# Side tasks of a hybrid decoder step: other waiting counts, earlier SSD blocks, gates one at a time, a fifth score buffer

## The chip, the cores and the metric

One core of a Trainium2 chip runs the whole kernel. The core has a matrix engine (TensorE, PE in the rows), two elementwise engines (VectorE, DVE, and ScalarE, ACT), GpSimd (POOL), and a queue engine (SyncE, SP) that issues nearly all DMAs. The metric is the device time of one execution in microseconds (us); the kernel before took 1676.14 us, the median of three runs from 1675.15 to 1676.15.

## The reference, cut to what matters

A decoder trunk of two layers in float32 handles a prompt of 1024 tokens and one new token for each of 8 samples. In each layer the residual x feeds one input projection whose outputs go to three mixers, and one output projection and a layer norm close the layer:

```
proj = x @ w_in            # 1024 -> 4876 columns
att  = sliding-window attention (window 128, 8 query heads, 2 key heads, sinks, partial rotary)
hl   = RG-LRU: conv(4) -> r, i = sigmoid(block matmuls) -> h_t = a_t h_{t-1} + b_t
y    = Mamba-2 SSD: conv(4)+silu on x, B, C -> chunked scan (chunks of 128) + D*x
y    = y * silu(z); y = y * rsqrt(mean(y^2)) * norm_g
out  = concat(att*silu(g_att), hl*silu(g_lru), y) @ w_out
x    = layer_norm(alpha * x + out)
```

The caches and states after the step are outputs too.

## The kernel before, in words

The work is done in four steps: for each of two layers, first half 0 (512 prompt tokens), then half 1 (512 prompt tokens and the 8 samples, 520 columns in two chunks of 260). Tokens lie along the free dimension and channels on partitions. A step projects 38 blocks of 128 output channels (`project`), then adds up the output projection in four groups of input rows (`out_proj`).

Every large product is taken as three float32r matmuls (`mac3`, lines 299 to 301: high weights by high x, high weights by low x, low weights by high x). These are the main products. ACT makes the high part of each weight tile (`wh`, lines 249 and 251), POOL the low part (`wl`, line 253); in half 1 the low part is read back from DRAM (`low`).

Everything else is a side task: a Python generator that emits some instructions and then yields a number. `pump()` is called once per slot, that is after every 12 main products in half 0 and every 24 shorter ones in half 1; it counts each task down and lets it emit its next piece when the count is used up. So a `yield 3` puts three slots of main products between two pieces of a task. `drain(...)` pumps without main products until the named streams are empty. What the generators emit is then placed on each engine by a scheduler that may shift instructions by some places; each engine runs its own list in order.

The side tasks that the change touches:

- Attention, `block` (line 845 on): scores into a `sp` tile (L855, L856 on PE, L859 on DVE, L863 on ACT), three slots, transposes (L873) and their copy into a second `sp` tile (L876 on DVE or L878 on ACT), one slot, then the product with the values (L884). `sp` has four buffers (`NS2`). `attention_sample` does the same for the samples (transposes of cached keys at L935).
- SSD step sizes, `rest` in `ssd_steps`: a cumulative sum (L539, L540), its negation on DVE (L543, tile `acs`), one slot, then its transpose on PE (L552), on which all SSD blocks rest.
- SSD, `block(g, b)` in `ssd_stream`: for each of two groups and four chunks, transposes (L627), decays (L643 on ACT, L644 on POOL, L650 on ACT, L652 on DVE, from a tile `acr` that a DMA broadcasts out of DRAM), three slots, the state and output products (L655, L660), and `finish` (L600, L602 on DVE), which multiplies with the z gate. A group starts when its block 7 has been projected: blocks 0 to 2 are x, 3 is B, 4 is C, 5 to 7 are the z gates. At the end the sums of squares (L613, L614), a reciprocal (L738) and six scalings (L742).
- RG-LRU, `lru_stream`: for each of six tiles the two gates on PE (L457) and ACT (L459), an elementwise chain (L464 to L485), and the product with the output gate. A tile starts only when its output gate (`g_lru`) is projected.
- `prepare_ssd`, `prepare_lru`, `past_rows`: tables of per-channel parameters, loaded once.

PSUM is evicted by DVE in the output projection (L1024) and for gates (L346), by ACT elsewhere (L332). Main products use three PSUM buffers (`ip`), side products five (`mm`). Large SBUF tiles (`u`) come from ten buffers; x, the mixers' inputs and the inputs of the output projection (`load_mix`, L229 on ACT and L230 on DVE) share them.

Of the kernel before, what the change touches and what calls it, by code (L numbers as in the profile page):

```python
# [14 lines left out]
ALU = mybir.AluOpType  # L15
AX = mybir.AxisListType

P = 128
# [14 lines left out]
LS = 41  # L33
SS = 29
NH = 5
NS2 = 4
# [14 lines left out]
def tile_trunk(ctx, tc, outs, x_t, cache_k, cache_v, st_lru_conv, st_ssd_conv, st_ssd_h, w_in, w_dt, w_out,  # L51
# [120 lines left out]
    def prepare_ssd():  # L172
        dma(ssd_p, ssd_cols)
        dma(dcol, ssd_d)
        for l in range(LAYERS):
            o = l * SS + 24
            V.tensor_scalar(ssd_p[:, :, o:o + 5], ssd_p[:, :, o:o + 5], 0.5, None, op0=ALU.mult)
        past_rows(past_s, ssd_p, 10, SS, 24)
# [11 lines left out]
    def prepare_lru():  # L190
        dma(lru_p, lru_cols)
        past_rows(past_l, lru_p, 6, LS, 32)

        spt = ctile([P, 5, 6 * LAYERS], "spt")
        lam = ctile([P, 6 * LAYERS], "lam")
        for l in range(LAYERS):
            o = l * LS + 37
            V.tensor_scalar(lru_p[:, :, o:o + 2], lru_p[:, :, o:o + 2], 0.5, None, op0=ALU.mult)
            V.tensor_scalar(lam[:, 6 * l:6 * l + 6], lru_p[:, :, l * LS + 39], -1.0, None, op0=ALU.mult)
# [168 lines left out]
    def past_rows(out, prm, n, per, wo):  # L368

        tmp = wtile([P, 10, NS], "sd", ND)[:, :n]  # L370
        for l in range(LAYERS):
            for t in range(3):
                to = out[:, l] if t == 0 else tmp
                V.tensor_tensor(to, prm[:, :, l * per + t:l * per + t + 22:3],
                                prm[:, :, l * per + wo + t, None].to_broadcast([P, n, NS]), ALU.mult)
                if t:
                    V.tensor_tensor(out[:, l], out[:, l], tmp, ALU.add)
# [34 lines left out]
    def lru_project(st, l, half, x, j, what):  # L412
# [6 lines left out]
        for i in range(3):  # L419
            t = 3 * j + i  # L420
            if what == 0:
                ps = project(l, x, W, B_XL + t)
                conv(ps, half, W, lru_p[:, t, :], l * LS + 32, past_l[:, l, t, :], halo_l[:, t, :], xc[:, i, :W],
# [11 lines left out]
    def lru_stream(st, l, half, mixrows):  # L435
# [3 lines left out]
        for j in range(2):  # L439
# [3 lines left out]
            yield 2  # L443
            xc = st["xc", j]
            for i in range(3):
                while ("lru", j, 1, i) not in st:
                    yield 1
                t = 3 * j + i
                gate = st["gt", j][:, i, :W]
                r, ig = wtile([P, WMAX], "hb", NH), wtile([P, WMAX], "hb", NH)  # L450
                for gi, dst in ((0, r), (1, ig)):
                    for cs in chunks(W):
                        ps = mm_tile()
                        n = cs.stop - cs.start
                        for k, c0, c1 in ((i, 0, 32), (i, 32, 64), (i, 64, 96), (3, 96, P)):
# [4 lines left out]
                                     bias=lru_p[:, t, o + 37 + gi:o + 38 + gi])  # L460
# [14 lines left out]
                if half:  # L475
                    V.tensor_tensor(t2[:, HALF:W], t2[:, HALF:W], lru_p[:, t, o + 24:o + 32], ALU.mult)
# [13 lines left out]
    def ssd_steps(st, l, half, x):  # L490
# [12 lines left out]
        def rest():  # L503
# [46 lines left out]
            yield 1  # L550
# [10 lines left out]
    def ssd_project(st, l, half, x, g, i):  # L561
# [6 lines left out]
        if i < 5:  # L568
# [3 lines left out]
            conv(ps, half, W, ssd_p[:, t, :], l * SS + 24, past_s[:, l, t, :], halo_s[:, t, :], dst,  # L572
# [17 lines left out]
    def ssd_stream(st, l, half, mixrows):  # L590
# [4 lines left out]
        def finish(g, cs, wd, yps):  # L595

            xb, zc = st["xb", g], st["zc", g]
            yd = wtile([P, 3, P], "sd", ND)
            for i in range(3):
                V.scalar_tensor_tensor(yd[:, i, :wd], xb[:, i, cs], dcol[:, l, 3 * g + i:3 * g + i + 1],  # L600
                                       yps[:, i, :wd], op0=ALU.mult, op1=ALU.add)
            V.tensor_tensor(zc[:, 0:3, cs], yd[:, :, :wd], zc[:, 0:3, cs], ALU.mult)  # L602
            left[g] -= 1
# [12 lines left out]
        def block(g, b):  # L616
# [53 lines left out]
            finish(g, cs, P, py[:, :384].rearrange("p (i q) -> p i q", i=3))  # L670

        def sample(g):
# [29 lines left out]
            finish(g, cs, NS, ysum)  # L702
# [29 lines left out]
        squares(1)  # L732
        for cs in chunks(W):
# [5 lines left out]
        for t in range(6):  # L739
            g, i = divmod(t, 3)  # L740
            zt = st["zc", g][:, i, :W]
            V.scalar_tensor_tensor(zt, zt, lru_p[:, t, l * LS + 40:l * LS + 41], ssq[:, :W],  # L742
# [95 lines left out]
    def attention_stream(st, l, half, mixrows, mixd0):  # L838
        W = HALF + NS * half

        def block(g, b, qa, ga):
# [37 lines left out]
            yield 1  # L879
# [30 lines left out]
        if half:  # L910
            spawn("att", keys_out())
            spawn("att", attention_sample(l, st["qs"], st["k_last"][:, P:], st["tab"][:, 2, :], st["gas"], mixd0))

    def attention_sample(l, qs, kn, vT, gas, mixd0):
# [7 lines left out]
        yield 1  # L922
# [8 lines left out]
        for i in range(2):  # L931
            kcT.append(wtile([P, 4, P], "sp", NS2))
# [355 lines left out]
```

## Time and profile before

| | before |
|---|---|
| median of three runs | 1676.14 us |
| the profiled execution | 1670.71 us, of it 1669.0 us from the first to the last instruction (the span) |
| mean granted TensorE clock | 0.976 of full |
| PE, DVE, ACT, POOL busy | 94%, 64%, 58%, 39% of the span |
| main products | 7776 of 10696 matmuls |
| DMA | 202 GB/s mean over the span |

A row of a timeline gives the start, the duration, the engine, the line, the operation, the output and inputs by the program's names, the shapes, a count, and in brackets how long the engine had been idle and what ended that. A PE record is longer than the time that a matmul takes of a stream, since records overlap; the rate is read from how many start in a stretch.

### The profile page before, as it was taken

The numbers are of one execution on the slowest core, as the hardware profiler recorded it, in microseconds if no ns is written. First come the engines' busy times: TensorE is split into PE (matmuls) and PEld (weight loads), VectorE is DVE, ScalarE is ACT, GpSimd is POOL, SyncE is SP. The second block draws the span as 40 slices with busy tenths as digits, with TensorE's granted clock in tenths as the row PEclk, the third lists the DMA queues.
The fourth block names the chain that finished last, engine by engine and source line by source line (L and its number), as shares of the span: only waits on it lengthen the run. The fifth ranks groups of instructions, "written<-read, shape, count | busy, mean of one in ns | idle before, by whom it ended". The sixth has DMA issues, their size and how long they took to land. (4 is left out here: it accounts for less than half of the span.)

```text
span 1669.0 us, 30988 instructions
## 1 busy us (share of the span) xinstructions
PE 1573.8 (94%) x10696; PEld 1340.7 (80%) x10696; DVE 1071.9 (64%) x2206; ACT 976.2 (58%) x2144; POOL 650.3 (39%) x858
## 2 busy tenths in 40 slices
PE   8999999999989999989998999988999998999996
PEld 6677776578989887879976777665899997978896
DVE  5656567855854766775488665679436557677734
ACT  5655566833555646783256564667346656578724
POOL 5654766463021354400155555665512105352000
PEclk9999999999989999999999999999999999999998
DMA  8655555986554666687546555568865556676965
GB/s 277 192 172 162 164 167 159 310 267 192 169 176 148 210 199 185 208 278 261 190 135 218 180 155 151 155 188 303 267 217 191 159 169 204 187 211 186 326 202 197
DMA packets 210660, 337.43 MB, mean 202 GB/s; under 512 B 24116, under 2 KB 64000, under 8 KB 210456
## 3 DMA queue, kind: packets, MB, share of 16 engines
q1 hardware_dynamic: 208200, 331.27, 62.5%
q10 hardware_dynamic: 2304, 4.20, 0.7%
q8 instruction: 84, 1.38, 0.3%
q14 instruction: 72, 0.59, 0.1%
HBM read 242.76 MB, written 92.05 MB: 201 GB/s over the span
## 5 line engine op out<-in xcount | busy, mean ns | idle before, releaser
L299 PE MATMUL ip<-u,wh 128*128 128x260 f32 (+3 forms) x2592 | 852.2, 329 | 31.6 <-DVE u L1024 15.1
L301 PE MATMUL ip<-u,wl 128*128 128x260 f32 (+3 forms) x2592 | 838.3, 325 | 13.2 <-DMA wl<-low 7.8
L300 PE MATMUL ip<-u,wh 128*128 128x260 f32 (+3 forms) x2592 | 838.1, 324 | 0.0
L299 PEld LDWEIGHTS ip<-u,wh 128*128 128x128 f32 x2592 | 495.9, 191 | 90.8 <-DVE u L1024 19.7
L301 PEld LDWEIGHTS ip<-u,wl 128*128 128x128 f32 x2592 | 494.2, 191 | 58.3 <-POOL wl L253 10.6
L300 PEld LDWEIGHTS ip<-u,wh 128*128 128x128 f32 x2592 | 496.3, 191 | 38.7 <-issue 3.2
L253 POOL TENSOR_TENSOR wl<-wraw,wh 128x256 fp32r<-128x256 f32 x432 | 374.1, 890 | 279.2 <-ACT wh L251 190.0
L249 ACT ACTIVATE wh<-wraw 128x512 fp32r<-128x512 f32 x224 | 138.7, 627 | 160.5 <-PE ip L300 130.2
L251 ACT ACTIVATE wh<-wraw 128x512 fp32r<-128x512 f32 x216 | 134.7, 627 | 148.5 <-PE ip L300 79.3
L1024 DVE SCALAR_TENSOR_TENSOR u<-u,ip 128x260 f32<-128x260 f32 (+3 forms) x192 | 96.7, 510 | 149.0 <-PE ip L301 147.3
L362 DVE SCALAR_TENSOR_TENSOR u<-ev,ssd_p,u 128x512 f32<-128x512 f32 x120 | 98.3, 820 | 19.2 <-ACT u L354 18.3
L863 ACT ACTIVATE sp<-sp,mx 128x257 f32<-128x257 f32 (+1 forms) x128 | 62.6, 491 | 42.6 <-DVE mx L859 42.6
L643 ACT ACTIVATE cq<-acr 128x384 f32<-128x384 f32 x56 | 29.2, 522 | 99.1 <-DMA acr<-acsd 88.7
L644 POOL TENSOR_TENSOR cq<-cq,u 128x384 f32<-128x384 f32 x56 | 63.8, 1140 | 51.7 <-ACT cq L643 33.4
L650 ACT ACTIVATE acr<-acr,acs 128x128 f32<-128x128 f32 x192 | 63.2, 393 | 33.5 <-POOL acr L647 30.7
L230 DVE TENSOR_TENSOR u<-u 128x512 fp32r<-128x512 f32 (+1 forms) x88 | 66.9, 785 | 17.6 <-ACT u L229 17.4
L362 DVE SCALAR_TENSOR_TENSOR u<-ev,lru_p,u 128x512 f32<-128x512 f32 x72 | 60.9, 846 | 24.8 <-ACT u L354 24.5
L229 ACT ACTIVATE u<-u 128x512 fp32r<-128x512 f32 (+1 forms) x88 | 52.3, 626 | 33.1 <-DMA u<-xd 14.9
L332 ACT ACTIVATE ev<-ip 128x260 f32<-128x260 f32 (+2 forms) x132 | 58.4, 443 | 17.9 <-PE ip L301 17.5
L457 PE MATMUL mm<-u,gw 96*32 96x260 f32 (+1 forms) x576 | 56.1, 468 | 13.4 <-ACT q L634 7.4
L652 DVE TENSOR_TENSOR acr<-acr,q 128x384 f32<-128x384 f32 x64 | 40.8, 669 | 42.2 <-ACT q L638 28.5
L859 DVE CUSTOM_DVE_ANT_0 sp<-mm,amask,sp 128x256 f32<-128x256 f32 (+1 forms) x128 | 54.6, 463 | 11.7 <-PE mm L856 10.5
(280 smaller groups left out, 2125.0 us busy)
## 6 DMA issues: line engine op xcount, KB each, us to landing
wraw<-in_w_in_dram SPq DMA_DIRECT2D x304, 256.0 KB
wl<-low SPq DMA_DIRECT2D x224, 256.0 KB
low<-wl SPq DMA_DIRECT2D x216, 256.0 KB
wraw<-in_w_out_dram SPq DMA_DIRECT2D x136, 256.0 KB
acr<-acsd SPq DMA_DIRECT2D x64, 192.0 KB
u<-mixd SPq DMA_DIRECT2D x32, 260.0 KB
u<-mixd SPq DMA_DIRECT2D x32, 256.0 KB
mixd<-u SPq DMA_DIRECT2D x24, 260.0 KB
```

The lines of the kernel that those rows point to most:

```text
L230: V.tensor_tensor(dl, raw, dh.bitcast(F32), ALU.subtract)
L249: S.activation(h, raw, AF.Copy)
L251: S.activation(h, raw, AF.Copy)
L253: G.tensor_tensor(low[:, c], raw[:, c], h[:, c].bitcast(F32), ALU.subtract)
L299: PE.matmul(out, wh, xh, start=first, stop=False)
L300: PE.matmul(out, wh, xl, start=False, stop=False)
L301: PE.matmul(out, wl, xh, start=False, stop=last)
L362: V.scalar_tensor_tensor(out[:, :HALF], raw[:, t:t + HALF], prm[:, wo + t:wo + t + 1], out[:, :HALF], op0=ALU.mult, op1=ALU.add)
L644: G.tensor_tensor(cq[i], cq[i], zc[:, None, 3, cs].to_broadcast([P, 3, P]), ALU.mult)
L650: S.activation(acr[i][:, e, :], acr[i][:, e, :], AF.Exp, scale=-1.0, bias=nacs[:, eb + 3 * i + e:eb + 3 * i + e + 1])
L863: S.activation(s[:, kv, :nk + 1], s[:, kv, :nk + 1], AF.Exp, scale=-1.0, bias=mx[:, kv:kv + 1], accum_out=den[:, kv:kv + 1])
L1024: V.scalar_tensor_tensor(ro, ro, ALPHA if gi == 0 else 1.0, out, op0=ALU.mult, op1=ALU.add)
```

## The change

Seven edits go together.

- Waiting counts: L552 comes 3 slots after L543 instead of 1 (in layer 1, half 0, the order has 36 main products between L540 and it, before 22); the value product L884 2 slots after the transposes instead of 1; the samples' transposes 4 slots after `prod` instead of 1, with a slot between the two key halves; `keys_out` starts after 8 slots instead of 3; RG-LRU waits 3 slots for its gate weights instead of 2; the mean square's product comes 2 slots after the last squares.
- SSD blocks of a group start at block 5 (x, B and C projected) instead of block 7. `finish` is cut in two: `weighted` right after the product, and the multiplication with z once block 7 is there. In layer 0, half 0, the last SSD products stand 48 main products earlier in PE's order.
- RG-LRU tiles start without their output gate and wait for it at the last product.
- The two gates of a tile are emitted one slot apart, and 3 slots (not 4) follow the tile.
- `NS2` is 5.
- The conv states' rows are no longer kept in SBUF with the parameters: `channel_rows` loads them into scratch (`hb`) tiles, in two parts for SSD and one for RG-LRU, and copies the parameters out. This frees 3072 bytes per partition (288 and 480 float32 columns).
- Line numbers differ: 299 to 301 are 295 to 297 in the changed kernel, 457 is 459, 229 is 225, 251 is 247, 655 and 660 are 667 and 672, 742 is 761, 346 is 342.

```diff
-NS2 = 4
+NS2 = 5
@@ prepare_ssd, prepare_lru
-        dma(ssd_p, ssd_cols)
...
-        past_rows(past_s, ssd_p, 10, SS, 24)
+        channel_rows(ssd_cols, 10, SS, 0, 0.5, ssd_p, past_s)
...
-        dma(lru_p, lru_cols)
-        past_rows(past_l, lru_p, 6, LS, 32)
+        channel_rows(lru_cols, 6, LS, 8, 1.0, lru_p, past_l)
@@
+    def channel_rows(cols, n, per, wo, scale, prm, past):
+        m = n if n * LAYERS * (ROWS + per) <= WMAX else n // 2
+        for t0 in range(0, n, m):
+            ts = slice(t0, t0 + m)
+            raw = wtile([P, WMAX], "hb", NH)[:, :m * LAYERS * (ROWS + per)].rearrange("p (t c) -> p t c", t=m)
+            dma(raw, cols[:, ts, :])
+            tmp = wtile([P, m, NS], "sd", ND)
...
@@ lru_stream
             dma(gw, gates_w[l, j])
-            yield 2
+            yield 3
             for i in range(3):
-                while ("lru", j, 1, i) not in st:
-                    yield 1
...
+                    if gi == 0:
+                        yield 1
...
+                while ("lru", j, 1, i) not in st:
+                    yield 1
+                gate = st["gt", j][:, i, :W]
                 V.scalar_tensor_tensor(gate, r, 0.5, gate, op0=ALU.mult, op1=ALU.mult)
-                yield 4
+                yield 3
@@ ssd_steps, rest
             V.tensor_tensor(dd, dd, dt[:, :48], ALU.mult)
-            yield 1
+            yield 3
@@ ssd_stream
-            finish(g, cs, P, py[:, :384].rearrange("p (i q) -> p i q", i=3))
+            yd = weighted(g, cs, P, py[:, :384].rearrange("p (i q) -> p i q", i=3))
+            while ("ssd", g, 7) not in st:
+                yield 1
+            finish(g, cs, P, yd)
...
-            while "steps" not in st or ("ssd", g, 7) not in st:
+            while "steps" not in st or ("ssd", g, 5) not in st:
                 yield 1
...
         squares(1)
+        yield 2
@@ attention
-            yield 1
+            yield 2
             po = mm_tile()
...
-            spawn("att", keys_out())
+            spawn("att", keys_out(), 8)
...
         V.tensor_tensor(prod, qs, kn[:, :, None].to_broadcast([P, NS, 8]), ALU.mult)
-        yield 1
+        yield 4
...
         for i in range(2):
+            yield 1
             kcT.append(wtile([P, 4, P], "sp", NS2))
```

What is executed stays the same but for 14 more small DVE instructions and one more DMA in the preparation, and 8 fewer table loads on ACT. The order moves. Three places follow, first before and then changed.

ACT, layer 0, half 0, before the output projection. L229 (225) is the first group's input (`u<-u`), L251 (247) the high weights, L613 (625) the SSD squares, L345 (341) the gates' evictions, L459 (461) to L469 (473) the RG-LRU chain. Before:

```order
L354 ACTIVATE u<-ev,lru_p 128x512
L229 ACTIVATE u<-u 128x512 x4
L251 ACTIVATE wh<-wraw 128x512
L613 ACTIVATE ev<-u 128x512 x3
L251 ACTIVATE wh<-wraw 128x512
L345 ACT_TABLE_LOAD
L345 ACTIVATE ev<-ip 128x512
```

Changed:

```order
L625 ACTIVATE ev<-u 128x512 x3
L247 ACTIVATE wh<-wraw 128x512
L328 ACTIVATE ev<-ip 128x512
L350 ACTIVATE u<-ev,lru_p 128x512
L247 ACTIVATE wh<-wraw 128x512 x2
L328 ACTIVATE ev<-ip 128x512
L350 ACTIVATE u<-ev,lru_p 128x512
L756 ACTIVATE ssq<-mm,eps_t 128x512
```

The squares stood behind L229 and now stand ahead of it, 18 rows before L225 x4, and the root of their sum (L756) with them.

PE, layer 0, half 0, the second RG-LRU tile. L457 (459) are the gates, the rest main products or SSD products. Before:

```order
L300 MATMUL ip<-u,wh 128x512
L301 MATMUL ip<-u,wl 128x512
L457 MATMUL mm<-u,gw 32x512 x8
L299 MATMUL ip<-u,wh 128x512
L300 MATMUL ip<-u,wh 128x512
L301 MATMUL ip<-u,wl 128x512
```

Changed, from the second gate on (the first stands 12 main products earlier, as another x4):

```order
L296 MATMUL ip<-u,wh 128x512
L297 MATMUL ip<-u,wl 128x512
L459 MATMUL mm<-u,gw 32x512 x4
L667 MATMUL mm<-sd,q 128x384
L672 MATMUL mm<-cq,hst_115 64x128 x2
L672 MATMUL mm<-acr,sd 64x128 x2
```

One group of eight became two of four. Over the whole program there are 27 such rows before and 48 after.

DVE, layer 0, half 1, around the start of the output projection. L742 (761) are the SSD scalings, L346 (342) the gates' evictions, L468 (472) to L485 (492) the RG-LRU chain, L1024 (1044) the evictions of the output projection. Before:

```order
L738 RECIPROCAL ssq<-ssq 128x520
L346 SCALAR_TENSOR_TENSOR u<-ev,ip 128x260
L742 SCALAR_TENSOR_TENSOR u<-u,lru_p,ssq 128x520 x6
L470 SCALAR_TENSOR_TENSOR hb<-hb,u 128x520
L468 SCALAR_TENSOR_TENSOR hb<-hb 128x520
L471 SCALAR_TENSOR_TENSOR hb<-hb 128x520
L346 SCALAR_TENSOR_TENSOR u<-ev,ip 128x260 x2
```

Changed:

```order
L757 RECIPROCAL ssq<-ssq 128x520
L358 SCALAR_TENSOR_TENSOR u<-ev,lru_p,u 128x512
L761 SCALAR_TENSOR_TENSOR u<-u,lru_p,ssq 128x520 x6
L474 SCALAR_TENSOR_TENSOR hb<-hb,u 128x520
L389 COPY q<-mm 66x128
L358 SCALAR_TENSOR_TENSOR u<-ev,lru_p,u 128x512
L472 SCALAR_TENSOR_TENSOR hb<-hb 128x520
L475 SCALAR_TENSOR_TENSOR hb<-hb 128x520
L342 SCALAR_TENSOR_TENSOR u<-ev,ip 128x260 x2
```

The scalings stand among the RG-LRU convolutions (L358) instead of between evictions of the last output gates.

## Rows read from the trace of the kernel before

**Rows 1.** The page, busy time by engine: us, share, instructions
```profile
PE 1573.8 (94%) x10696; PEld 1340.7 (80%) x10696; DVE 1071.9 (64%) x2206; ACT 976.2 (58%) x2144; POOL 650.3 (39%) x858
```

**Rows 2.** Clock of the core: span, mean granted share
```profile
core 0: 1669.0 us, clock 0.976
```

**Rows 3.** Waits of PE: instruction, releaser, us in total, times, longest
```profile
PE ip L299 <- DVE u L1024: 15.1, 12, 4.3
PE ip L299 <- ACT wh L251: 10.3, 4, 6.5
PE mm L884 <- ACT sp L878: 8.8, 3, 3.4
PE ip L301 <- DMA wl<-low: 7.8, 5, 2.9
PE mm L457 <- ACT q L634: 7.4, 4, 2.9
PE mm L457 <- DMA u<-u: 5.5, 3, 2.7
PE mm L552 <- DVE acs L543: 5.5, 2, 4.4
PE ip L301 <- POOL wl L253: 5.1, 4, 2.4
PE ip L299 <- DVE u L346: 4.7, 3, 2.3
PE mm L935 <- DVE sp L876: 3.4, 2, 2.2
```

**Rows 4.** Stretches: length, busy us (count) of each engine, PE clock, DMA
```profile
0.00:20.00 20.00, 13.49 (x47) 9.82 (x48) 11.50 (x24) 13.33 (x33) 13.12 (x32) 1.00 0.91 305
...
280.00:300.00 20.00, 16.16 (x64) 10.70 (x63) 13.08 (x18) 14.48 (x22) 10.22 (x10) 0.83 0.55 179
...
360.00:380.00 20.00, 20.00 (x88) 16.11 (x87) 4.82 (x7) 4.43 (x7) 9.51 (x14) 1.00 0.74 223
...
880.00:900.00 20.00, 15.58 (x61) 12.56 (x61) 19.12 (x39) 9.93 (x26) 9.39 (x12) 0.83 0.70 240
...
1400.00:1420.00 20.00, 13.20 (x107) 10.84 (x106) 16.33 (x49) 13.27 (x34) 11.29 (x14) 0.91 0.71 208
```

**Rows 5.** Timeline of PE from 281 to 288 us
```profile
283.84 0.50 PE L299 MATMUL ip<-u,wh 128*128 128x512 f32 x1 [1.47 <-ACT wh L251]
...
286.95 0.79 PE L301 MATMUL ip<-u,wl 128*128 128x512 f32 x1 [2.37 <-POOL wl L253]
```

**Rows 6.** Timeline of ACT from 262 to 287 us
```profile
281.08 2.19 ACT L229 ACTIVATE u<-u 128x512 fp32r<-128x512 f32 x4 [4.21 <-DVE sd L600]
```

**Rows 7.** Timeline of DVE from 270 to 287 us
```profile
280.71 0.34 DVE L600 SCALAR_TENSOR_TENSOR sd<-u,dcol,mm 128x128 f32<-128x128 f32 x1
```

**Rows 8.** Timeline of PE from 879 to 886 us
```profile
884.60 0.41 PE L552 MATMUL mm<-ident,acs 128*48 128x128 f32 x1 [4.42 <-DVE acs L543]
```

**Rows 9.** Timeline of DVE from 877 to 886 us
```profile
884.34 0.20 DVE L543 TENSOR_SCALAR acs<-mm 128x48 f32<-128x48 f32 x1
```

**Rows 10.** Waits of ACT: the longest sum with a DMA
```profile
ACT cq L643 <- DMA acr<-acsd: 88.7, 28, 6.7
```

**Rows 11.** Groups of ACT by line and shape: busy us, mean ns, idle before
```profile
L857 ACT ACTIVATE sp<-sink_bc 128x2 f32<-128x2 f32 x64 | 12.6, 198 | 0.6 <-PE mm L884 0.4 <-DVE sink_bc L136 0.2
```

**Rows 12.** Timeline of PE from 1491 to 1500 us
```profile
1491.24 0.28 PE L301 MATMUL ip<-u,wl 128*128 128x260 f32 x1
1491.45 1.52 PE L457 MATMUL mm<-u,gw 96*32 96x260 f32 x24
1495.85 0.65 PE L457 MATMUL mm<-u,gw 96*32 96x260 f32 x8 [2.88 <-ACT q L634]
1496.42 0.39 PE L299 MATMUL ip<-u,wh 128*128 128x260 f32 x1
```

**Rows 13.** Timeline of DVE from 716 to 739 us
```profile
735.78 0.70 DVE L468 SCALAR_TENSOR_TENSOR hb<-hb 128x520 f32<-128x520 f32 x1 [2.53 <-ACT hb L466]
```

More of the change, by code (lines that the diff above doesn't have):

```diff
@@ L32 @@
 B_K, B_V, B_Q, B_GA, B_XL, B_GL, B_Z, B_XBC = 0, 1, 2, 6, 10, 16, 22, 28
-LS = 41
-SS = 29
+LS = 17
+SS = 5
+ROWS = 24
 NH = 5
-NS2 = 4
+NS2 = 5
 NE = 5
@@ L172, in prepare_ssd @@
     def prepare_ssd():
-        dma(ssd_p, ssd_cols)
+        channel_rows(ssd_cols, 10, SS, 0, 0.5, ssd_p, past_s)
         dma(dcol, ssd_d)
-        for l in range(LAYERS):
-            o = l * SS + 24
-            V.tensor_scalar(ssd_p[:, :, o:o + 5], ssd_p[:, :, o:o + 5], 0.5, None, op0=ALU.mult)
-        past_rows(past_s, ssd_p, 10, SS, 24)
         G.memset(tri, 1.0)
@@ L366, in conv @@
             G.tensor_copy(last, raw[:, HALF:HALF + 11])
[L368 to L377, printed above, removed]
+    def channel_rows(cols, n, per, wo, scale, prm, past):
[5 more added lines that the diff above has]
+            tmp = wtile([P, m, NS], "sd", ND)
+            for l in range(LAYERS):
+                r0 = l * (ROWS + per)
+                V.tensor_scalar(prm[:, ts, l * per:(l + 1) * per], raw[:, :, r0 + ROWS:r0 + ROWS + per], scale, None,
+                                op0=ALU.mult)
+                for t in range(3):
+                    to = past[:, l, ts] if t == 0 else tmp
+                    V.tensor_tensor(to, raw[:, :, r0 + t:r0 + t + 22:3],
+                                    prm[:, ts, l * per + wo + t, None].to_broadcast([P, m, NS]), ALU.mult)
+                    if t:
+                        V.tensor_tensor(past[:, l, ts], past[:, l, ts], tmp, ALU.add)
     def rows_out(src, m, dsts):
@@ L422, in lru_project @@
                 ps = project(l, x, W, B_XL + t)
-                conv(ps, half, W, lru_p[:, t, :], l * LS + 32, past_l[:, l, t, :], halo_l[:, t, :], xc[:, i, :W],
+                conv(ps, half, W, lru_p[:, t, :], l * LS + 8, past_l[:, l, t, :], halo_l[:, t, :], xc[:, i, :W],
                      last_l[:, :, t])
@@ L571, in ssd_project @@
             ps = project(l, x, W, ssd_block(g, i))
-            conv(ps, half, W, ssd_p[:, t, :], l * SS + 24, past_s[:, l, t, :], halo_s[:, t, :], dst,
+            conv(ps, half, W, ssd_p[:, t, :], l * SS, past_s[:, l, t, :], halo_s[:, t, :], dst,
                  last_s[:, :, t])
@@ L593, in ssd_stream, with weighted @@
         left = {}
-        def finish(g, cs, wd, yps):
-            xb, zc = st["xb", g], st["zc", g]
+        def weighted(g, cs, wd, yps):
+            xb = st["xb", g]
             yd = wtile([P, 3, P], "sd", ND)
@@ L601, in finish @@
                                        yps[:, i, :wd], op0=ALU.mult, op1=ALU.add)
+            return yd
+        def finish(g, cs, wd, yd):
+            zc = st["zc", g]
             V.tensor_tensor(zc[:, 0:3, cs], yd[:, :, :wd], zc[:, 0:3, cs], ALU.mult)
@@ L701, in sample @@
                 yield 1
-            finish(g, cs, NS, ysum)
+            while ("ssd", g, 7) not in st:
+                yield 1
+            finish(g, cs, NS, weighted(g, cs, NS, ysum))
         def final_state(g):
@@ L741, in ssd_stream @@
             zt = st["zc", g][:, i, :W]
[L742 removed]
+            V.scalar_tensor_tensor(zt, zt, lru_p[:, t, l * LS + 16:l * LS + 17], ssq[:, :W],
                                    op0=ALU.mult, op1=ALU.mult)
@@ L931, in attention_sample @@
         for i in range(2):
+            yield 1
             kcT.append(wtile([P, 4, P], "sp", NS2))
```

9 lines of the change are left out of this document (4 added, 5 removed).

## The prediction

> **What bounds the kernel now.** The page comes first: PE is busy 94% of the span, the next engine 64% [rows 1]. So the end is set by PE's stream, and an edit counts only where it closes a hole in that stream or lengthens it. What an undisturbed stream does is in the table of stretches: from 360 to 380 us PE starts 88 products of 512 columns, one in 0.227 us, at the full clock [rows 4]. A slot of 12 is therefore 2.7 us. From 1400 to 1420 us it starts 107 matmuls and is busy only 13.2 us [rows 4]: one of the holes.
>
> Who makes the holes is in the list of PE's waits [rows 3]. They fall into five kinds, and only four have to do with this change: weights that ACT and POOL finish late (L251, L253), the transpose of the SSD sums (L552), products whose operand has just been copied (L884, L935), the RG-LRU gates (L457), and PSUM evictions that DVE does late (L1024, L346). The low weights from DRAM (7.8 us) wait for a transfer that nothing here moves. Of the 10.3 us for L251, the longest, 6.5 us, is the start of the program, when PE has nothing to do yet.
>
> A hole costs twice. In the stretch from 280 to 300 us, which holds two weight waits, the granted clock is 0.83, from 880 to 900 us, after a wait of 4.42 us, 0.83, from 1400 to 1420 us 0.91 [rows 4, 8]. There are two levels, 2.4 and 1.2 GHz, so 0.83 over 20 us is 6.8 us at the lower one, and what the stream loses is at most (1 - 0.83) x 20 = 3.4 us; at 0.91 it is 1.8 us. Over the span (1 - 0.976) x 1669 = 40 us is the most that all of this can be [rows 2]; I use 1.8 to 3.4 us for each hole that closes.
>
> **The change part by part**, against the profiled execution (1670.7 us; the median of the runs is 5.4 us above it, and I add that at the end).
>
> *SSD blocks start earlier (weights at the output projection).* At 281 us ACT has stood idle for 4.21 us in front of L229, the input of the output projection [rows 6]. What it waited for is L600, which ends at 281.05 us [rows 7]: the tile that L229 writes is the SSD input that L600 still reads. Behind L229 in ACT's order stands L251, the high weights, and PE then waits 1.47 us for them and 2.37 us for the low part that POOL makes of them [rows 5]. In the new order the last SSD products of this half stand 48 main products earlier, 48 x 0.227 = 10.9 us, which is more than the 4.21 us; the tile is free when L225 comes. Both layers have this place: without the program's start, [rows 3] has 10.3 - 6.5 = 3.8 us for L251 and 5.1 us for L253, together 8.9 us, and two drops of the clock. What is late next: the RG-LRU chain, which I leave in the last term. Between 0 and 8.9 + 5.2 = 14.1 us; I take 11.
>
> *Three slots before the SSD transpose.* DVE works through a queue of long normalisation steps and comes to L543 at 884.34 us; PE, which stands at L552, waits 4.42 us, with all main products behind it [rows 8, 9]. Now 36 main products instead of 22 lie between: 14 x 0.227 = 3.2 us, and the score products that stand there too are some more. Of the two waits (5.5 us in all [rows 3]), the short one goes, the long one shrinks to about 1 us, and the clock stays: 1.1 + 3.2 + 2.4 = 6.7 us. The blocks that rest on this transpose start up to 2 slots later, which the earlier start of the groups hides; without that cover it would take back the 2.7 to 5.4 us.
>
> *One slot more before L884, and between the samples' pieces.* Three waits of L884, 8.8 us, the longest 3.4 us, and two of L935, 3.4 us [rows 3]. A slot takes 2.7 us from each: 8.8 would shrink to about 1.4 us, L935 to nothing. That would be 10.8 us and three drops of the clock, 16 us. But what makes ACT late is not distance alone: it stands in front of L643 for the broadcast of `acr` 88.7 us in all, up to 6.7 us at a time [rows 10], and the change leaves that DMA in the same step as its reader; SP issues it earlier together with its block, past weight loads. So between 0 and 16 us; I take 9. The fifth score buffer is priced at nothing: the instruction that opens a new score tile (L857) waited 0.4 us for L884 with four [rows 11], and with tiles held one slot longer the fifth keeps it there.
>
> *Gates one at a time, tiles without their output gate.* The waits are 7.4 us for L634, which empties a PSUM buffer that the gates need, and 5.5 us for the shifted rows (`u<-u`) [rows 3]. One more slot before the first gate is 2.7 us against a longest wait of 2.7 us; half as many PSUM buffers are asked for at once. With some four drops of the clock the most is 12.9 + 8 = 21 us. ACT's order is still that of [rows 10], so I take half, 10.4 us.
>
> Against it stands a sure cost. A gate's chunk is 8 records. The last one alone, from its start to the next main product, takes 1496.42 - 1495.85 = 0.57 us; three of them (24 records) start 1491.45 us and, at the same rate with one exit, give about 0.44 us each, so leaving costs 0.13 us; entering takes 0.21 us (1491.24 to 1491.45) instead of 0.12 us [rows 12]. Each extra group is 0.22 us; the order has 48 instead of 27: 21 x 0.22 = 4.6 us. Bounds: 0 (where the group stands beside SSD products that change the shape anyway) and 21 x 0.57 = 12 us.
>
> The Trainium skill has a rule here: "TensorE: Matmul & The Clock Gate", Part 3, says that packed small matmuls take the duration of one plus about 4 ns for each further tile, and names no cost of entering or leaving; by it the split would cost nothing and the sum would be 4.6 us better. The rows above show the entry and the exit as time, so they decide.
>
> *Evictions.* DVE does the six SSD scalings, the RG-LRU chains and the evictions L346 and L1024 in one queue at the start of the output projection. At 735.78 us it stands 2.53 us for ACT in front of L468, with L1024 behind it [rows 13], and the longest wait of PE for L1024 is 4.3 us; L1024 and L346 together make 19.8 us [rows 3]. In the new order the scalings are done among the convolutions, before the output gates. But the RG-LRU chain ends later, since a tile now takes the same slots and its start is bound by the tile before; L472 still stands in front of L1044. Between -5 (the chain meets more of the evictions) and 19.8 + 4 = 24 us; I take half, 12.
>
> *Preparation.* 14 more small DVE instructions and one more DMA; at 0.20 us for a small one [rows 9] 2.8 us. In the first 20 us DVE is busy 11.5 us [rows 4], so they hide; 0, at worst 2.8.
>
> *New waits.* In half 1 the samples' SSD work of group 0 now falls on the last attention groups, where it did not before. From 1400 to 1420 us, where such work met before, PE lost 6.8 us [rows 4]. No row shows the new meeting; between 0 and two such holes (13.6 us and clock 3.6) I take 7 for the two layers, one half of a hole each.
>
> Sum: 11 + 6.7 + 9 + 10.4 + 12 - 4.6 - 7 = 37.5 us; 1670.7 - 37.5 = 1633, and with the 5.4 us to the median 1638 us.
>
> **The rivals.**
>
> *Only the certain part comes.* Waits on ACT and DVE are waits on queues, and a queue that is late for one product may be late for the next whatever the slots. [Rows 10] speaks for it (ACT's idle time in front of L643 is not touched), the ends of L543 and L600 against it for those two places. Then 11 + 6.7 - 4.6 = 13 us remain: 1663 us.
>
> *Nearly all of it comes.* If the waits hang on bunching alone and the even order removes it: 14.1 + 8.9 + 16 + 21 + 24 - 4.6 = 79 us, 1597 us. For it: the order spreads scores and value products over alternate slots. Against: the chain of RG-LRU in the output projection is no shorter.
>
> *Slower.* In half 1 the SSD samples, SSD blocks and attention together overfill DVE. From 880 to 900 us DVE was busy 19.1 of 20 us and PE lost 4.4 us; from 1400 to 1420 us 6.8 us [rows 4]. If three such stretches in each layer stand where one stood, with the clock: 2 x 3 x (6.8 + 1.8) = 52 us more, against about 40 us that the rest gains: 1688 us. It decides from the point where DVE is over 18 us busy in three or more stretches of 20 us between the first scores of group 3 and the last SSD block of group 0. Against it: DVE's work in total grows by 2.8 us only, and was 64%.
>
> *The parts cancel.* Split groups at their bound (12 us) and new holes (17 us) eat the small gains: 1676 us.
>
> **How the numbers follow.** Forecast (1622 to 1655 us) 0.52, only the certain part 0.22, nearly all 0.12, cancel 0.05, slower 0.09. A difference of 0.2%, 3.4 us, is what a measurement of this kernel can tell. Faster by more than that: 0.86, within it 0.05, slower 0.09. The range 1600 to 1672 us leaves about a tenth on either side.
>
> **What would show it.** In the profile after: no idle time of ACT in front of L225 at the output projection, and no wait of PE for L247 but the first; the wait for the SSD transpose under 1.5 us in all; L884's product waiting less than 3 us; entries into gate groups 0.2 us each at 48 places; the granted clock above 0.976. Wrong would be: PE busy under 16 us in several stretches of half 1 around the samples, or the sum of PE's waits unchanged with other names.

## The result, and the profile after

The changed kernel takes 1659.63 us (median of 4 runs, 1656.27 to 1660.85) against 1676.14 us: ratio 0.990, 95% interval 0.988 to 0.992, so 16.5 us or 1.0% faster. A second comparison gave 0.988 (0.985 to 0.991). The direction and the range held; the forecast saving of 38 us is more than twice the measured one. The profiled execution took 1659.71 us with a span of 1658.0 us.

The page and the core's line after, to hold beside [rows 1, 2]:

```profile
PE 1573.9 (95%) x10696; PEld 1335.0 (81%) x10696; DVE 1066.0 (64%) x2220; ACT 965.0 (58%) x2136; POOL 642.7 (39%) x858
```

```profile
core 0: 1658.0 us, clock 0.978
```

PE does the same work in 11 us less span. The waits of PE after (instruction, releaser, us in total, times, longest) answer to [rows 3]:

```profile
PE ip L295 <- DVE u L1044: 13.0, 11, 3.7
PE ip L295 <- ACT wh L247: 9.1, 2, 6.6
PE ip L297 <- DMA wl<-low: 7.4, 8, 3.8
PE ip L295 <- DVE ga L342: 7.2, 2, 5.7
PE mm L982 <- DVE dg L979: 7.0, 1, 7.0
PE mm L982 <- ACT ev L341: 6.2, 1, 6.2
PE mm L903 <- DVE sd L607: 5.6, 2, 3.0
PE mm L892 <- DVE sp L885: 4.9, 2, 4.7
PE mm L903 <- ACT sp L897: 3.2, 3, 2.3
PE ip L297 <- POOL wl L249: 1.1, 2, 1.0
...
PE mm L559 <- DVE acs L550: 0.7, 1, 0.7
```

Lines have moved: L299 is now L295, L1024 is L1044, L457 is L459, L552 is L559, L884 is L903, L873 is L892. Gone are both waits of the gates (12.9 us in [rows 3]), nearly all of the wait for POOL's low weights (5.1 to 1.1) and for the SSD transpose (5.5 to 0.7). In their place stand names that the list before did not have: L982, L903 for L607, L892 for L885, L295 for `ga`. All listed waits together are 80.8 us before and 69.2 after. A second profile of the changed kernel lists 62.3 us, of them 7.9 for L1044, so a row of a single list is good to some 5 us only.

L982 is the product in the samples' attention that reads what the softmax leaves. Its first wait ends at 655.86 us (timeline of PE), and DVE's own timeline from 649 to 656 us shows why (start, us, instruction):

```profile
655.86 0.37 PE L982 MATMUL mm<-dg,bsel 64*8 64x64 f32 x2 [6.18 <-ACT ev L341]
```

```profile
649.12 0.14 DVE L974 TENSOR_TENSOR sm<-sm 64x1 f32<-64x1 f32 x1
...
651.05 0.14 DVE L975 TENSOR_SCALAR sm<-sm 64x1 f32<-64x1 f32 x1
...
653.51 0.15 DVE L976 RECIPROCAL sm<-sm 64x1 f32<-64x1 f32 x1
...
654.84 0.60 DVE L977 TENSOR_SCALAR spr<-spr,sm 64x129 f32<-64x129 f32 x1
655.47 0.25 DVE L979 TENSOR_SCALAR dg<-ident,spr 64x64 f32<-64x64 f32 x1
```

Five small steps, 1.3 us of work, take 6.6 us, since between the first four of them DVE's order has SSD work (L607, L681, L614, L642, L644), sample states (L714), convolutions (L358) and an eviction (L342). ACT's L341, which the list names, ended at 652.1 us; DVE's L979 came last. In just these 6.6 us DVE is busy all the time (length, then busy us and count of PE, weight loads, DVE, ACT and POOL, clock, DMA share, GB/s):

```profile
649.12:655.72 6.60, 0.56 (x5) 0.35 (x3) 6.57 (x24) 4.28 (x13) 4.77 (x6) 0.70 0.48 152
```

At the second wait, from 1463 to 1470 us, it is busy 6.11 of 7 us, and for 0.89 us its queue stands for POOL (L711) between two steps of the chain. The stretches with the two waits, and those of [rows 4] again in the same columns:

```profile
280.00:300.00 20.00, 19.61 (x91) 14.08 (x90) 15.31 (x22) 11.62 (x20) 13.67 (x10) 1.00 0.72 242
...
640.00:660.00 20.00, 12.46 (x91) 10.01 (x90) 15.71 (x51) 10.85 (x31) 10.85 (x12) 0.79 0.72 229
880.00:900.00 20.00, 15.25 (x65) 11.85 (x66) 17.09 (x39) 12.59 (x32) 9.86 (x14) 0.83 0.73 223
...
1400.00:1420.00 20.00, 19.93 (x179) 18.44 (x178) 13.29 (x30) 14.59 (x37) 5.52 (x8) 1.00 0.55 169
1460.00:1480.00 20.00, 12.99 (x103) 10.14 (x102) 12.41 (x44) 8.49 (x23) 6.42 (x8) 0.83 0.59 183
```

The holes at 280 and 1400 us have closed, with the clock at its upper level; new ones stand at 640 and 1460 us, with it at the lower level for part of the stretch. At 880 us nothing changed but the name: PE stands at L892, for L885 behind the same normalisation (L1091) on DVE that held L552 [rows 8, 9].

```profile
889.88 0.69 PE L892 MATMUL mm<-ident,sp 128*128 128x128 f32 x2 [4.71 <-DVE sp L885]
```

### The profile page after: what moved, and what is told of

Same layout as the page of the kernel before. It is cut to its first block, busy times and chain, and to the rows that moved or that the text cites. A ratio compares the mean times of both kernels' runs of the same rounds, so it can differ in the third digit from the quotient of the medians.

```text
span 1658.0 us, 31019 instructions
## 1 busy us (share of the span) xinstructions
PE 1573.9 (95%) x10696; PEld 1335.0 (81%) x10696; DVE 1066.0 (64%) x2220; ACT 965.0 (58%) x2136; POOL 642.7 (39%) x858
## 4 chain that ended last, share of the span: by engine, by line
PE 62%; DVE 12%; DMA 10%; ACT 6%; issue 3%; POOL 2%; SPq 1%; DVEq 0%; ACTq 0%; POOLq 0%
PE ip L295 17%; PE ip L297 17%; PE ip L296 17%; PE mm L459 2%; PE mm L672 2%; PE mm L903 2%; PE mm L892 2%; DVE u L358 1%; DMA wl<-low 1%; DVE sd L714 1%; DMA out_dram<-h 1%; DMA wraw<-in_w_out_dram 1%; PE mm L667 1%; ACT wh L245 1%; DMA h<-in_st_ssd_h_dram 1%
## 5 line engine op out<-in xcount | busy, mean ns | idle before, releaser
L295 PE MATMUL ip<-u,wh 128*128 128x260 f32 (+3 forms) x2592 | 853.0, 329 | 30.4 <-DVE u L1044 13.0
L295 PEld LDWEIGHTS ip<-u,wh 128*128 128x128 f32 x2592 | 494.6, 191 | 93.3 <-issue 22.6
L249 POOL TENSOR_TENSOR wl<-wraw,wh 128x256 fp32r<-128x256 f32 x432 | 369.7, 880 | 253.2 <-ACT wh L247 173.2
L1044 DVE SCALAR_TENSOR_TENSOR u<-u,ip 128x260 f32<-128x260 f32 (+3 forms) x192 | 96.8, 509 | 136.9 <-PE ip L297 132.2
L358 DVE SCALAR_TENSOR_TENSOR u<-ev,ssd_p,u 128x512 f32<-128x512 f32 x120 | 101.1, 843 | 14.6 <-ACT u L350 12.4
L226 DVE TENSOR_TENSOR u<-u 128x512 fp32r<-128x512 f32 (+1 forms) x88 | 64.7, 763 | 31.2 <-ACT u L225 31.0
L358 DVE SCALAR_TENSOR_TENSOR u<-ev,lru_p,u 128x512 f32<-128x512 f32 x72 | 63.6, 886 | 19.9 <-ACT u L350 10.7
L878 DVE CUSTOM_DVE_ANT_0 sp<-mm,amask,sp 128x256 f32<-128x256 f32 (+1 forms) x128 | 54.5, 462 | 33.2 <-PE mm L875 10.4
L342 DVE SCALAR_TENSOR_TENSOR u<-ev,ip 128x260 f32<-128x260 f32 (+1 forms) x72 | 36.4, 507 | 58.4 <-ACT ev L341 58.3
L225 ACT ACTIVATE u<-u 128x512 fp32r<-128x512 f32 (+1 forms) x88 | 52.1, 626 | 31.3 <-DMA u<-mixd 18.1
L714 DVE CUSTOM_DVE_ANT_0 sd<-bb,h 128x128 f32<-128x128 f32 x96 | 38.0, 443 | 37.8 <-POOL h L711 35.0
```

What stands on the lines that cost most here:

```text
L226: V.tensor_tensor(dl, raw, dh.bitcast(F32), ALU.subtract)
L249: G.tensor_tensor(low[:, c], raw[:, c], h[:, c].bitcast(F32), ALU.subtract)
L295: PE.matmul(out, wh, xh, start=first, stop=False)
L358: V.scalar_tensor_tensor(out[:, :HALF], raw[:, t:t + HALF], prm[:, wo + t:wo + t + 1], out[:, :HALF], op0=ALU.mult, op1=ALU.add)
L1044: V.scalar_tensor_tensor(ro, ro, ALPHA if gi == 0 else 1.0, out, op0=ALU.mult, op1=ALU.add)
```

## Experiments

Each ratio is to the kernel before, run on the same chip. The changed kernel itself lies at 0.988 to 0.990, so a single undoing is read against that. One kernel's runs spread by some 0.4% to either side, and an interval reaches 0.001 to 0.003 to either side. The experiments ran on several chips, so from one to another it is the ratios that are compared. Where lines were taken out or moved, numbers differ by up to 4 (L1042 for L1044, L462 for L459).

**Where do the new waits come from?** Five slots in place of two in front of L982:

```
         V.tensor_scalar(dg, ident[:64, :64], ...)
-        yield 2
+        yield 5
         pd = mm_tile()
```

> The changed kernel (1659.6 us), with five slots in place of two between the samples' softmax and the product that reads it (L982). Theory A, new waits took the place of the ones removed: PE waits 13.2 us in all for this product in the changed kernel, 6.2 us at 649 us and 7.0 us at 1463 us, and the granted clock falls to one half behind both (10.2 and 6.8 us of it, which costs about half as much). With more slots both go and the time falls by 13 to 21 us, to 1639 to 1647 us. Theory B, a wait only moves along the queues: VectorE and ScalarE are behind there anyway, the next product that needs them waits as long, and the time stays within 4 us of 1659.6.

Measured: 0.9852 (0.9826 to 0.9877). L982 has left the list, yet the gain is 4 to 7 us and not 13 to 21: the gates now wait 9.2 us for the shifted rows (`u<-u`) four main products later. The result lies between the theories, and its interval overlaps that of the changed kernel's second measurement (0.9848 to 0.9907).

Then the samples' slots as before (`yield 4` to `yield 1` after the first step, no `yield 1` between the transposes, no 8 slots for `keys_out`), beside the changed kernel once more:

> The changed kernel once more, beside the next three on one chip and with the same runs of the kernel before. Both theories: the ratio to the kernel before is that of the first comparison, 0.988 to 0.992. It is the measure for the single edits, since the times of one kernel differ by some microseconds from chip to chip.

> The changed kernel with the samples' attention as early as before (one slot in place of four after its first step, none between the two groups of transposes, and three in place of eight in front of the last key rows). Theory A: the five slots moved the samples' softmax into the stretch where the second group's SSD blocks, now earlier, keep VectorE busy; earlier, L982 waits less than 3 us in all (13.2 us in the changed kernel) and the time is 6 to 12 us under the changed kernel. Theory B: it then meets the first group's blocks, and the transposes of the cached keys come before their data: within 4 us of the changed kernel.

Measured in one comparison: changed kernel 0.9877 (0.9848 to 0.9907), slots undone 0.9824 (0.9799 to 0.985), medians 1653.62 and 1642.50 us. L982 is not in the list of waits any more; here too the gates wait in its place, 6.8 us. So the samples' added slots, the three edits together, cost about 10 us. That this comes from where they put the softmax is what the trace shows; the late `keys_out` was not undone alone.

**The slots in front of the SSD transpose, and of L903.**

```
-            yield 3
+            yield 1
             pa = mm_tile()        # steps_undone, L559
...
-            yield 2
+            yield 1
             po = mm_tile()        # values_undone, L903
```

> The changed kernel with one slot in place of three before the transpose of the SSD steps (L559). Recorded term 2: 6.7 us are lost again, 1666 us, as the transpose waits for L550 behind the norm's work on VectorE at 884 us and in the other three stages. Theory A: in the changed kernel the attention's transposes (L892) wait 4.7 us at 884 us for that same work of VectorE; with the transpose put back it is L559 that waits there and L892 no longer, so the sum of both waits is the same and only the smaller waits of the other stages come back: 1660 to 1663 us.

> The changed kernel with one slot again between the attention's transposes and the product with the values (L903). Recorded term 3 (a gain of 9 us, most of it here): the waits for L897 come back, 8 us slower than the changed kernel, ratio to the kernel before 0.995. Theory A (the wait is one for ScalarE and VectorE, which are behind with other work, so half of it is met elsewhere): 2 to 5 us slower than the changed kernel, 0.991 to 0.993.

Measured: 0.9865 (0.9841 to 0.989), 2 to 5 us faster and inside the intervals, and 0.9923 (0.9902 to 0.9945). Of steps_undone the list of waits has

```profile
PE mm L903 <- ACT sp L897: 7.0, 3, 5.7
...
PE mm L559 <- DVE acs L550: 5.4, 2, 4.4
...
PE mm L892 <- ACT sp L886: 1.1, 1, 1.1
PE ip L295 <- DVE ga L342: 1.0, 1, 1.0
```

where the changed kernel has 3.2 for L897, 0.7 for L550, 4.9 for L885 (of which steps_undone has no row) and 7.2 for `ga`. Both long waits only change their owner. The 4.4 us on DVE's norm are L559's in one kernel and L892's in the other. The wait for `ga` stands at main product 1729 of the changed kernel, and one main product later steps_undone waits as long at L903; first the changed kernel, then steps_undone:

```profile
466.05 0.59 PE L295 MATMUL ip<-u,wh 128*128 128x260 f32 x1 [5.70 <-DVE ga L342]
```

```profile
461.81 1.12 PE L903 MATMUL mm<-sp,vtok 128*64 128x128 f32 x8 [5.71 <-ACT sp L897]
```

So what makes the time 2 to 5 us shorter, if it is, these rows do not show. Undoing L903's slot costs 4 to 8 us, and the intervals (0.9902 to 0.9945, 0.9848 to 0.9907) just overlap: its wait for L897 comes back (8.6 us).

**Do the undoings add?**

> The changed kernel with both edits that came out faster alone: five slots in front of the samples' product L982 and one slot again in front of the SSD steps' transpose L559. Alone they gave ratios of 0.985 and 0.987 to the kernel before. Theory A (separate waits, each at its own place: L982 at 649 and 1463 us, L559 and L892 at 884 us): the gains add, ratio 0.980 to 0.983, 7 to 9 us under the better of the two. Theory B (a wait moves along the queues): no better than the better one, 0.984 to 0.987.

> The changed kernel without the two parts that came out as harmful: the samples' attention as early as before, and one slot before the SSD steps' transpose. Alone the two undoings gave ratios of 0.982 and 0.987 to the kernel before, where the changed kernel has 0.988 to 0.990. Theory A (separate waits, each at its own place, gains add): 0.977 to 0.980, 34 to 38 us under the kernel before, which is the saving forecast for the change. Theory B (a wait moves along the queues): 0.982 to 0.985.

Measured: 0.9806 (0.9781 to 0.9832) and 0.9797 (0.9781 to 0.9813). This is what gains that add would give, though the interval of the second still overlaps that of the samples' slots alone (0.9799 to 0.985). The second is the changed kernel without the samples' slots and without those of the SSD transpose; its median is 1643.84 us against 1677.09 in the same comparison, 33 us, and no version here is faster than it by more than the intervals. Its core line:

```profile
core 0: 1642.2 us, clock 0.983
```

**What carries the gain?** First the SSD start (`("ssd", g, 5)` back to 7) and the RG-LRU part (gates together, wait for the output gate in front, slots 2 and 4), each undone in the changed kernel:

> The changed kernel with the start of the SSD blocks put back to the eighth input block. Recorded term 1: 11 us are lost again, 1671 us, with ScalarE idle in front of L225 at the first tile of the out-projection of half 0. Theory A: of the gain seen at the start of the out-projections of half 0 (7.4 and 9.5 us) 7 us each are given back inside the out-projections in the changed kernel; without the early start both the gain and the giving back go, and the blocks of the second group no longer stand beside the samples' softmax, so that the waits for L982 shrink: within 5 us of 1659.6.

> The changed kernel with the RG-LRU part undone: both gates of a tile together, behind the tile's output gate, with 2 and 4 slots as before. Theory A (new waits took the place of old ones): the gates' waits come back (12.9 us in the kernel before), but the two waits in the out-projection of half 0 (L295 for an evicted tile of L1044, 3.7 us each with a fall of the clock behind each) go, as the RG-LRU chain ends earlier: the sum is within 5 us of 1659.6. The recorded term 4 (a gain of 10 us, 5 for the single gates counted against it): 1665 to 1675 us. If single gates cost what the split was priced at (4.6 us) and give nothing: 1655 us.

Measured: 0.9979 (0.9963 to 0.9995) and 0.9989 (0.9974 to 1.0004): 14 to 17 us and 15 to 19 us lost. Without the early start (the profile is of an execution 7.5 us above the median) PE waits 12.9 us for the sum of squares, which neither the kernel before nor the changed one does, and L982 11.4; without the new gates 15.4 us for L342, and the waits for L1044 are down to 2.8. Theory A of both, that gain and giving back cancel, is wrong.

The RG-LRU part in pieces: both gates in one slot (the `if gi == 0: yield 1` removed), the same with `yield 4` behind the tile so that its period stays at four slots, and the split kept with the wait for the output gate in front:

> The changed kernel with both gates of a tile in one slot again, all else as changed (so the wait for the output gate stays late and the slots stay 3 and 3). The recorded split cost: 21 groups of 0.22 us fewer, 4.6 us faster, ratio 0.985 to 0.987. By the packed-matmul rule (no cost of a further group): the same as the changed kernel, 0.988 to 0.990. Theory A: the split also spreads the demand for PSUM buffers and for ScalarE, so that with both together the waits of L459 for ScalarE (none in the changed kernel, 7.4 us in the kernel before) come back: 0 to 5 us slower, 0.990 to 0.993.

> The changed kernel with both gates in one slot, and four slots in place of three behind a tile, so that a tile takes four slots as in the changed kernel (in gates_together it took three, and the ratio was 1.001). Theory A (the split itself spreads what PE, ScalarE and the PSUM buffers are asked for in one slot): most of the loss stays, 0.996 to 1.001. Theory C (the number of slots for a tile is what counts, since a shorter period puts the RG-LRU chains on top of the SSD blocks): back to the changed kernel or better, 0.985 to 0.991. The recorded split cost adds 4.6 us to C: 0.985 to 0.987.

> The changed kernel with the wait for a tile's output gate in front of its gates, as before, the split and the slots as changed. lru_undone (together and wait in front) had 0.999. Theory A (the split carries the gain): 0.988 to 0.992. Theory D (the later wait carries it, because gates and chains of the first tiles stand in front of the output gates' products and the chain ends earlier): 0.995 to 0.999, and the chain's DVE work meets the evictions of the out-projection again, with waits of PE for L342 as in lru_undone (15.4 us).

Measured: 1.0011 (0.9997 to 1.0025), 0.9951 (0.993 to 0.9972), 0.9882 (0.986 to 0.9904). So the late wait is worth nothing beside the split, the split 9 to 12 us, and a tile in three slots instead of four costs another 10. Between lru_undone and gates_together_4 lie 6 us more, for the late wait or the third slot in front of the gates; no run separates these two. From the starts of PE's records I summed what PE spends on gate groups, waits in front of and behind them included: 82.2 us in 26 groups before, 80.2 in 40 (lru_undone), 81.6 in 32 and 83.8 in 46 (the two with both gates together), and 64.1 and 65.5 in 48 groups with the split (changed kernel, split_wait_early). The scheduler thus breaks groups apart in every changed version. The price of a group itself was right: a single gate in half 0 (8 records) takes 1.00 us, two together 1.85, and an entry 0.09 more than the step to another main product, so two single ones cost 0.24 us more. From before to the changed kernel PE's idle time at the groups falls from 24.4 to 1.1 us, and the rest rises from 57.8 to 63.1, 0.24 us for each of 22 groups. Between gates_together_4 and split_wait_early it is otherwise: idle time falls only from 9.6 to 2.6 us, the rest from 74.2 to 63.0, and the lists of waits have the same sum (67.6 and 67.7). Part of it is where a group is cut. One of a gate's four products (two records) takes as long by itself as all four, here in the changed kernel:

```profile
235.46 1.07 PE L459 MATMUL mm<-u,gw 96*32 96x512 f32 x8
...
315.81 1.05 PE L459 MATMUL mm<-u,gw 96*32 96x512 f32 x2
```

To the next main product it is 1.00 and 0.98 us. Of such single products gates_together_4 has 12, split_wait_early 6; at 0.98 us in half 0 and 0.56 in half 1 the difference is an estimated 5 of these 11 us. Two waits of gates_together_4, which split_wait_early has not or under 1 us:

```profile
PE mm L459 <- DMA u<-u: 5.1, 2, 2.7
...
PE ip L295 <- DVE u L342: 3.1, 1, 3.1
```

**What does the rest do?** The SSD start, the gates and all slots as before except the two behind the last squares; the early start added to that; a `yield 2` near the squares removed, in the best version and in the first; four score buffers, in both. The `yield 2` that was removed is not the one of the change:

```
                 squares(0)
-        yield 2          # removed; the kernel before has it too
         while left[1]:
             yield 1
         squares(1)
         yield 2          # of the change; it stays in every run here
```

The expectations of three_parts_out and layout_squares_out take it for the other.

> The changed kernel with all slots, the gates and the start of the SSD blocks as before, so that the parameters by rows (L364), the fifth score buffer, the split of the SSD blocks' last step and the two slots in front of the sum of squares remain. Recorded terms: 0 to 2.8 us slower for the preparation and nothing for the buffer, ratio 1.000 to 1.002. Theory A adds up the single undoings (SSD start 14 us, gates 15 us, slot before L903 8 us gained; samples' slots 9 us, slots before L559 5 us lost: 23 us gained) against the 20 us measured in the same comparison, which leaves 3 us lost here: 1.000 to 1.004. If the buffer has a share of its own in the gain: 0.994 to 0.998.

> The kernel of layout_only with the earlier start of the SSD blocks as the one part more. Theory A (parts add, and each has its own place): the 14 us that its undoing cost are gained here too, ratio 0.009 below that of layout_only. Recorded term 1: 11 us, 0.0066 below it. Theory B (the gain needs the later gates, because the RG-LRU chain meets the evictions in the out-projection otherwise): under 5 us, within 0.003 of it.

> The kernel of two_parts_out (0.980) without the two slots in front of the last sum of squares as well. If these slots are what makes layout_only slower than the kernel before (7 us), 0.975 to 0.978. If their cost is bound to the old order of the gates, where the squares fall on the start of the out-projection: 0.979 to 0.982.

> The kernel of layout_only (1.004) without the two slots in front of the last sum of squares: what remains of the change is the layout of the parameters, the fifth score buffer and the split of the blocks' last step. If the slots cost the 7 us: 0.999 to 1.001. If the parameters' preparation or the buffer does: 1.003 to 1.005; the preparation was bounded at 2.8 us, 0.0017.

> The kernel of layout_squares_out (1.004) with four score buffers as before. If the fifth buffer costs the 7 us, because a new score tile then no longer holds ScalarE and VectorE back and they run on into other work in front of what PE waits for: 0.999 to 1.001. If the parameters by rows or the split last step cost it: 1.003 to 1.005.

> The kernel of two_parts_out (0.980) with four score buffers. With three and two slots in the attention's chain a score tile is held one slot longer than before. If the fourth buffer then comes free too late (the reason for a fifth): PE waits in front of L874, 0.984 to 0.990. If the fifth buffer is without effect here, as the recorded price of nothing says: 0.978 to 0.982. If it costs what layout_only lost: 0.975 to 0.977.

Measured, in this order: 1.0042 (1.0027 to 1.0057), 1.0044 (1.0027 to 1.006), 0.9824 (0.981 to 0.9838), 1.0044 (1.0031 to 1.0057), 1.0046 (1.0024 to 1.0067), 0.9809 (0.9784 to 0.9834). So the early SSD start alone gives nothing. That it needs the split gates fits the lists (with it alone L342 waits 15.8 us, as in lru_undone, against 3.8 in layout_only), but no run adds just these two. The older slots and the fifth buffer have no effect that these runs can tell. The three runs without the other parts (layout_only, layout_squares_out, layout_four_buffers) are 7 to 8 us slower than the kernel before. What they share, and it has not, are the parameters by rows and the two slots behind the last squares; the block's last step in two pieces does nothing there, since block 7 is already projected when a group starts.

The traces tell where the 7 us arise. The 865th main product, at 276.7 us before, starts 0.1 us later in layout_four_buffers (1.4 and 1.8 us in layout_only and layout_squares_out), so the preparation costs little. In the output projections of half 1 PE's longest waits for an eviction (L1041 or L1040) grow from 4.3 and 3.4 us to 6.4 and 7.4 (layout_four_buffers; 6.4 and 6.6 in layout_only), 6 of the 8 us by which the profiled spans of layout_four_buffers and before differ. There DVE waits for the x that a DMA brings back, first before, then in layout_four_buffers:

```profile
737.89 1.09 DVE L1024 SCALAR_TENSOR_TENSOR u<-u,ip 128x260 f32<-128x260 f32 x3 [0.80 <-DMA u<-in_x_t_dram]
```

```profile
740.64 1.10 DVE L1040 SCALAR_TENSOR_TENSOR u<-u,ip 128x260 f32<-128x260 f32 x3 [3.07 <-DMA u<-in_x_t_dram]
```

SP issues that load 4.5 us later than before (733.83 against 729.37 us). In its order an output of the SSD state (L726), for which it waits until 728.77 us, now stands between the writes of the SSD scalings (L760), and the load behind them all; before, the state's output came after these writes. The two slots behind the squares give such other tasks two more turns ahead of the scalings, so these slots are the likelier cause. No run takes them out, and the cause stays open.

## Why the prediction was right and wrong

The direction was right, and the sum failed in three steps. A wait was counted as gained where only its owner changed (SSD transpose) or where what it waits for stayed late (evictions). The place to which the samples' task moves was not looked at. And no term had the 7 us that remain as a loss when the other parts are out. That the time came out near the rival "only the certain part" (1663 us) is luck: of its three terms 6.7 came out near -4, and the -4.6 belongs to the best part of the change.

*SSD start* (11 us): right at its place. ACT's first input of the output projection no longer waits for DVE (the row has no idle time, unlike [rows 6]):

```profile
283.22 2.18 ACT L225 ACTIVATE u<-u 128x512 fp32r<-128x512 f32 x4
```

Undoing it cost 14 to 17 us, the largest row of which (12.9 us for the sum of squares) is no wait of the kernel before. But the term was priced as if it stood alone, and alone it is 0: POOL's 5.1 us go there too, and L342 waits instead.

*Three slots before the SSD transpose* (6.7 us): this step failed. Its own wait went as forecast, but PE's next instruction that reads DVE stood in the same queue behind the same norm: 4.7 us of L892 in place of 4.4 of L552. Undone, the time is no longer but 2 to 8 us shorter (0.9865 against 0.988 to 0.990, inside the intervals; 0.9806 against 0.9852, just at their ends).

*L903 and the samples' pieces* (9 us): one half right, 4 to 8 us for L903 against the 8.8 us of waits there; that its product waits under 3 us was wrong, since 5.6 us for L607 came. The other half has the wrong sign: the samples' slots cost 10 us. The text looked at the wait that the slots remove (L935, 3.4 us) and not at what stands at the place to which they move the rest of the task.

*Gates* (10.4, less 4.6 for the split): the waits went. Netting 15 to 19 us instead of 5.8, this is the best part. The split's own price was 0.22 us for a group, measured 0.24, but the split was counted against the change and it carries 9 to 12 us of the gain. The cited rule of the Trainium skill ("TensorE: Matmul & The Clock Gate", Part 3) would have had it cost nothing, where the trace shows 0.24 us; neither price holds the waits, nor what a cut inside a gate costs.

*Evictions* (12 us): this step failed too. L1024 and L346 had 19.8 us; L1044 and the `ga` and `u` rows of L342 have 20.6, in the second profile 14.5, so the gain lies between -1 and 5 us. As the text feared, the chain of RG-LRU meets them: from 333 to 337.6 us DVE does L472, L475, L476 and the next inputs' low parts (L226) while L1044 stands behind, and with the RG-LRU part undone the waits for L1044 are 2.8 us.

*New waits* (-7 us): of the right kind, too small. L982 alone is 13.2 us, with two falls of the clock (0.79 and 0.83 in 20 us, at most 4.2 + 3.4 us); both stretches are under 16 us of PE, which the text had named as a sign of being wrong. The rival "slower" looked for such places by DVE over 18 us busy in 20, and here it has 15.71 and 12.41. The thought was right, the measure too coarse: while the first chain lasts DVE is busy 6.57 of 6.60 us, and it idles elsewhere in the 20.

*Preparation* (0, at worst 2.8): it costs 0.1 to 1.8 us up to 277 us. Of the change without its other parts 7 us of loss remain, most of them at the output projections of half 1, where no term had them.

The sum by what the runs show: about 15 (SSD start) + 17 (gates) + 6 (L903) - 10 (samples) - 4 (SSD transpose, inside the noise) - 7 (rest) = 17, near the measured 16.5 to 20. The parts depend on each other, so this is an account and no proof. The forecast's 38 us is nearly reached, 33, by the version without the two parts that had been counted as gains.

## What to carry to other kernels

Slots between a producer and its reader move everything behind them as well: look at what stands at the new place, and above all for chains of small steps that cross a shared in-order queue, where each step pays the queue once. Read an engine's busy share over the wait itself, not over a stretch three times as long. A wait for a queue that is late anyway goes to the next reader, so count it as gained only if the queue's work moves. Undo each part alone before taking a gain in the sum for a gain in each part.

## What was not expected of the hardware

One small gate product alone holds PE for 0.98 us, four of them together for 1.00, so where a group is cut matters more than how often. A gate group's wait was worth more than its entry: with 22 more groups, some 5 us at 0.24 each, PE's idle time at them fell by 23 us. One kernel's runs on one chip differ more than the first comparison showed: 1644 to 1659 us for the changed kernel in the second one.
